# A hybrid decoder layer: head drawn into the ordered first stage, six merge products with gates ahead of the copies, other PSUM side for the FFN, last row tile in two column parts

## The chip, the cores and the metric

The program runs on one core of a Trainium2 chip. The metric is the device time of one execution in microseconds (us), lower is better. Beside times there is the trace of one profiled execution. Its engines are PE (TensorE, matmuls; PEld is its weight load), DVE (VectorE), ACT (ScalarE), POOL (GpSimd) and SP (SyncE, which here issues the transfers). Each engine takes its instructions in the order of its own queue, and waits at one whose inputs aren't ready.

## The reference, cut to what matters

One decoder layer on 512 tokens of width 1024: an input projection feeds two causal mixers, whose outputs are projected, gated by channel, merged, projected again, added to the input and normalized; then a gated FFN with a short convolution, and again a normalization.

```python
h = x @ w_in
y_a = nsa_attention(q, k.., v.., gates, ..) @ w_nsa_out        # 8 heads of 64, three branches
y_b = gated_deltanet(qkv, beta, decay, gate, ..) @ w_gdn_out   # 4 heads of 128, chunks of 64
gate_a, gate_b = split(merge_gate)                             # 2 x 1024 columns of h
mix = (sigmoid(gate_a) * y_a + sigmoid(gate_b) * y_b) @ w_o
x = layer_norm(ALPHA * x + mix, ln1_g, ln1_b)
gate, val = split(causal_dwconv(x @ w_up, conv_w))             # 2 x 2816 columns, width 3
x = layer_norm(ALPHA * x + (silu(gate) * val) @ w_down, ln2_g, ln2_b)
```

Everything is float32.

## The kernel before

**Products.** A float32 operand is split into a high part in the matmul type (float32r) and the rest (`xh`, `xl`; `wh`, `wl`). A product is three matmuls: high by high, high by low, low by high. Weights come by DMA into one of three `raw` buffers; `split_w` (L361) makes `wh` (mostly on ScalarE) and `wl` (VectorE or GpSimd), each with three buffers. `gemm_t(u)` (L396) is 24 matmuls of 512 columns into one of the two PSUM banks `pg`: unit u, 128 columns of the input projection, for all 512 tokens. Its weight is called `w<u>` in the order below (w20, w18, ...).

**The head.** After eight idle matmuls on zeros (`still`), `token_major` (L410) loads the eight x tiles (256 KB each) and four weight tiles `wB` (288 KB), splits them, and makes 96 matmuls of 288 columns into four banks `pb`, one for each tile of 128 tokens. They hold the columns that are wanted token by token (v, gates, decays); small copies take them out (`vcat`, `gsig`, `bd`). Then seven SyncE transfers bring constants: `cst` (722 KB), `ident` and small rows (L467 to L490). The Tile scheduler orders all this.

**The ordered stage.** From there to the end of both mixers, `draw(name, f)` runs a step only to record its instructions for each engine, and the loop at L1014 gives them out as the table `GIVEN` says: `w20S` is the next SyncE instruction of step w20, `q0P*12` twelve TensorE instructions of step q0, `n0V@2` the third VectorE instruction of n0. `PLACE` says which buffer each tile takes. Instructions of this stage have line L1023, of all others L252, since helpers make them. Merge products are steps of this stage too: `g0` to `g6` are seven of the 16 gate products; the gate itself (`gate`, a tanh on ScalarE that empties the pg bank into `mt`) belongs to the step for the first `BUFS["mg"]` = 5.

**The merge** (L1026 to L1075): eight outputs of the mixers (`oT`, `yT`) are copied to `yoh`, of which six on ScalarE, and the rests to `yol`. Behind these in the program stand the gates of products 5 and 6. Then, for each of m = 0..7: gate products, up to four ahead, two output products of 12 matmuls into the two banks `pm`, and their merging on VectorE and ScalarE into `mh`, `ml`; in between weights for `w_o` are split.

**Behind it**: `w_o` (tiles `pw`), transposes (`pt`), the first normalization; FFN-up with `pu`; FFN-down, where products of sums (`tdn` holds sums of weights, made through `traw` buffers and stored to DRAM) go into `pdna` and `pdnb`, four banks. `mul` (L1277) takes 11 blocks, loaded by twos; `early` puts the split weights of the first two into `wh`/`wl`, the others into `dh`/`dl`. At the end the last product is done for row tile 0 and then 1, six blocks each, followed by `add`, statistics and `norm`, which stores 512 columns twice.

PSUM has eight banks. Before: `pg` 0 and 1, `pb` 2 to 5, then `pd` 2 and 3, `pa` 4 to 6, `po` 7; `pm` 2 to 5; `pu` 0 to 3, `pw` 4 and 5, `pt` 6 and 7; `pdn` 4 to 7.

## Time and profile before

| | us |
|---|---|
| median of 3 runs (lowest, highest) | 832.1 (831.31, 832.76) |
| the profiled execution: whole time | 835.69 |
| its span | 833.9 |
| mean granted TensorE clock | 0.992 |

The span goes from the first to the last recorded instruction. The stages in the trace:

| stage | from, us | to, us |
|---|---|---|
| head | 0 | 20.9 |
| ordered stage | 20.9 | 328.4 |
| merge | 328.4 | 429.1 |
| w_o and first normalization | 429.1 | 484.0 |
| FFN-up | 484.0 | 718.5 |
| FFN-down | 718.5 | 825.8 |
| tail | 825.8 | 833.9 |

Rows of the profile name the line, the engine, the operation and the tiles, written left of `<-` and read right of it. "x48" is a count. In brackets stands the idle time ahead and what ended it.

### The profile page before, as it was taken

What the parts mean: (1) busy time and instruction counts of PE and PEld (TensorE: products, weight loads), DVE (VectorE), ACT (ScalarE), POOL (GpSimd) and SP (SyncE); (2) the same over time, 40 slices, a digit from 0 to 9 for tenths busy, and PEclk for the clock granted to TensorE, in tenths of its full rate; (3) what the DMA queues carried; (4) which work ended last, traced back from release to release, by engine and by line L of the source; (5) the groups of instructions that cost most, each with busy time, mean ns of one, the idle gap of its engine ahead of it and who ended that gap; (6) DMA issues with size and microseconds to landing.
All of it is one profiled execution on the core that took longest, in us unless ns stands there. A gap on an engine that the chain in (4) does not pass through costs nothing.

```text
span 833.9 us, 12016 instructions
## 1 busy us (share of the span) xinstructions
PE 813.7 (98%) x4226; PEld 685.5 (82%) x4226; DVE 636.8 (76%) x1373; ACT 403.8 (48%) x916; POOL 143.5 (17%) x127
## 2 busy tenths in 40 slices
...
GB/s 276 97 85 102 51 51 51 26 27 88 65 27 66 29 36 74 97 160 124 151 200 154 16 61 103 186 186 190 194 202 202 202 202 209 208 219 200 265 197 103
DMA packets 39820, 108.06 MB, mean 130 GB/s; under 512 B 4560, under 2 KB 4944, under 8 KB 39504
## 3 DMA queue, kind: packets, MB, share of 16 engines
...
q8 instruction: 33, 0.54, 0.3%
...
## 4 chain that ended last, share of the span: by engine, by line
PE 86%; DVE 6%; DMA 4%; ACT 2%; issue 2%; POOL 0%; SPq 0%; DVEq 0%; ACTq 0%; POOLq 0%
PE pu L252 27%; PE pg L1023 20%; PE pd L1023 7%; PE pg L252 6%; PE pa L1023 5%; PE pm L252 5%; PE pdna L252 5%; PE pdnb L252 4%; PE pw L252 3%; PE po L1023 3%; DMA raw<-in_down 2%; DVE x L252 1%; DVE wl L252 1%; DMA raw<-in_wT 1%; DMA big<-in_xT 1%
## 5 line engine op out<-in xcount | busy, mean ns | idle before, releaser
L252 PE MATMUL pu<-mh,wh 128*128 128x512 f32 (+1 forms) x384 | 142.7, 372 | 0.0
L252 PE MATMUL pu<-ml,wh 128*128 128x512 f32 (+1 forms) x384 | 142.6, 371 | 0.0
L252 PE MATMUL pu<-mh,wl 128*128 128x512 f32 (+1 forms) x384 | 142.6, 371 | 0.0
L252 ACT ACTIVATE wh<-raw 128x512 fp32r<-128x512 f32 (+2 forms) x120 | 75.5, 632 | 110.7 <-PE pu L252 70.0
L252 DVE TENSOR_TENSOR wl<-raw,wh 128x512 fp32r<-128x512 f32 (+2 forms) x116 | 93.7, 810 | 37.2 <-ACT wh L252 37.0
L1023 PE MATMUL pg<-xh,wh 128*128 128x512 f32 x248 | 100.2, 407 | 1.8 <-ACT wh L1023 1.8
L1023 PE MATMUL pg<-xl,wh 128*128 128x512 f32 x248 | 99.2, 401 | 0.0
L1023 PE MATMUL pg<-xh,wl 128*128 128x512 f32 x248 | 97.7, 399 | 0.0
L252 PEld LDWEIGHTS pu<-ml,wh 128*128 128x128 f32 x384 | 72.3, 188 | 12.6
L252 PEld LDWEIGHTS pu<-mh,wh 128*128 128x128 f32 x384 | 72.3, 188 | 12.6
L252 PEld LDWEIGHTS pu<-mh,wl 128*128 128x128 f32 x384 | 72.3, 188 | 12.3
L252 DVE SCALAR_TENSOR_TENSOR fa<-pu,fcw,fa 128x511 f32<-128x511 f32 x88 | 65.7, 746 | 9.3 <-ACT fa L252 7.9
L252 POOL TENSOR_TENSOR fth<-fth,fa 128x512 f32<-128x512 f32 x22 | 29.5, 1340 | 214.1 <-DVE fa L252 199.9
L252 DVE TENSOR_TENSOR dl<-raw,dh 128x512 fp32r<-128x512 f32 x69 | 46.6, 705 | 18.4 <-ACT dh L252 18.2
L252 ACT ACTIVATE dh<-raw 128x512 fp32r<-128x512 f32 x69 | 41.7, 627 | 35.4 <-DVE dl L252 10.4
L1023 PEld LDWEIGHTS pg<-xh,wh 128*128 128x128 f32 x248 | 47.1, 190 | 10.7 <-ACT wh L1023 2.0
L1023 ACT ACTIVATE big<-big,mn 128x384 f32<-128x384 f32 (+3 forms) x84 | 45.6, 554 | 21.1 <-DVE mn L1023 20.3
L1023 PEld LDWEIGHTS pg<-xh,wl 128*128 128x128 f32 x248 | 46.9, 190 | 8.9 <-DVE wl L1023 0.4
L1023 PEld LDWEIGHTS pg<-xl,wh 128*128 128x128 f32 x248 | 47.0, 189 | 8.3
L1023 POOL TENSOR_TENSOR wl<-raw,wh 128x512 fp32r<-128x512 f32 x28 | 36.3, 1306 | 80.6 <-ACT wh L1023 49.7
L252 POOL TENSOR_TENSOR rs<-rs,minus_half 128x1 f32<-128x1 f32 x8 | 7.5, 942 | 166.1 <-DVE rs L252 166.1
L252 PE MATMUL pg<-xh,wh 128*128 128x512 f32 x72 | 29.4, 408 | 5.3 <-ACT mt L252 5.3
...
## 6 DMA issues: line engine op xcount, KB each, us to landing
...
tdn<-traw SPq DMA_DIRECT2D x44, 256.0 KB, 3.1
...
```

Source lines behind the costliest of these rows:

```text
L252: return give(*a, **kw)
L1023: give(*a, **kw)
```

## The change

- The head is drawn too: `token_major(k0)` as steps t0, t2, t4, t6, the copies out of its banks as u, the constants as z; the table gives their places. The first x tile and the first wB tile come in halves, and for k0 = 0 VectorE makes the high part. The four accumulators are tiles of `pd` and `pa`.
- `GIVEN` and `PLACE` are new for the whole ordered stage; the steps in it are the same but for the head and the gate g5.
- `BUFS["mg"]` is 6: six gates belong to the ordered stage, and three gate products stand ahead of the first output product instead of two. The leftover gate (product 6) is written ahead of the yoh copies.
- `pu` lies on the right side of PSUM (banks 4 to 7), so `pw` takes the banks of `pg`, `pt` 2 and 3, `pdn` 0 to 3.
- FFN-down: blocks 2 and 3 of the first product go into tiles `eh`, `el` of a new pool `tl`, where the `traw` buffers were.
- The last row tile is multiplied in two halves of the last 512 columns, the second into a bank of its own; its statistics have three parts, its first normalizing pass is one operation of 1024 columns, the second three (512, 256, 256), each stored by itself.

Three places show the moved instructions. First SyncE, from the last x tile of the head on (`big` holds x tiles; the first `raw<-in_wT` is w20). Before:

```order
L252 DMA big7_94<-in_xT 128x512
L252 DMA cst_350<-in_consts 128x1444
L252 DMA ident_352<-in_consts 128x128
L252 DMA gcw_358<-in_gcw 128x48
L252 DMA fcw_360<-in_fcw 128x132
L252 DMA gnw_363<-in_gnw 128x1
L252 DMA alog_366<-in_glog 128x4
L252 DMA gdt_368<-in_gdt 128x4
L1023 DMA raw1_157<-in_wT 128x1024
```

The same place after the change:

```order
L1044 DMA big7_94<-in_xT 128x512
L1044 DMA raw1_157<-in_wT 128x1024
L1044 DMA gdt_208<-in_gdt 128x4
L1044 DMA raw2_158<-in_wT 128x1024
L1044 DMA gcw_204<-in_gcw 128x48
L1044 DMA raw0_156<-in_wT 128x1024
L1044 DMA raw1_157<-in_wT 128x1024
L1044 DMA raw2_158<-in_wT 128x1024
L1044 DMA pos_242<-in_pos 128x32
L1044 DMA alog_207<-in_glog 128x4
L1044 DMA raw1_157<-in_wT 128x1024
L1044 DMA cst_200<-in_consts 128x1444
```

w20 now follows x at once, and cst stands behind six weight loads. Second ScalarE, from the last copy of the ordered stage (`big<-po`) on; `mt` are gates. Before:

```order
L1023 ACTIVATE big22_109<-po0_398 64x512
L252 ACTIVATE yoh_3281<-oT_429 128x512
L252 ACTIVATE yoh_3281<-oT_432 128x512
L252 ACTIVATE yoh_3281<-yT_424 128x512
L252 ACTIVATE yoh_3281<-yT_426 128x512
L252 ACTIVATE yoh_3281<-yT_427 128x512
L252 ACTIVATE yoh_3281<-yT_435 128x512
L252 ACTIVATE mt_3311<-pg1_172 128x512
L252 ACTIVATE mt_3313<-pg0_171 128x512
```

And after the change:

```order
L1044 ACTIVATE big2_89<-po0_182 64x512
L1044 ACTIVATE mt_260<-pg0_183 128x512
L261 ACTIVATE mt_3285<-pg1_184 128x512
L261 ACTIVATE yoh_3279<-oT_253 128x512
L261 ACTIVATE yoh_3279<-oT_256 128x512
L261 ACTIVATE yoh_3279<-yT_248 128x512
L261 ACTIVATE yoh_3279<-yT_250 128x512
L261 ACTIVATE yoh_3279<-yT_251 128x512
L261 ACTIVATE yoh_3279<-yT_259 128x512
```

Both gates moved ahead of the six copies. Third ScalarE at the start of FFN-down (`dh`, `eh` are high parts of weights, `h` parts of the FFN's inner values, `fa` the last of FFN-up). Before:

```order
L252 ACTIVATE fa1_6232<-pu1_6207,fcw_360 128x512
L252 ACTIVATE dh_6281<-raw1_157 128x512
L252 ACTIVATE dh_6285<-raw1_157 128x512
L252 ACTIVATE dh_6302<-raw2_158 128x512
L252 ACTIVATE dh_6306<-raw2_158 128x512
L252 ACTIVATE h11_4488<-s3_4500 128x512
L252 ACTIVATE dh_6323<-raw0_156 128x512
L252 ACTIVATE h12_4490<-fth_6236 128x256
```

And after the change:

```order
L261 ACTIVATE fa1_6228<-pu1_6203,fcw_205 128x512
L261 ACTIVATE dh_6301<-raw2_158 128x512
L261 ACTIVATE eh2_6280<-raw1_157 128x512
L261 ACTIVATE eh3_6284<-raw1_157 128x512
L261 ACTIVATE dh_6305<-raw2_158 128x512
L261 ACTIVATE h11_4484<-s3_4496 128x512
L261 ACTIVATE dh_6322<-raw0_156 128x512
L261 ACTIVATE h12_4486<-fth_6232 128x256
```

Block 4's high part (first `dh<-raw2`) went ahead of those of blocks 2 and 3, which are `eh` now. The diff, with the two tables cut to a line or two and longer hunks to their core:

```diff
 GIVEN = """
-w20S w20A w20V w20A w20V n0V@2 q0P*12 w18S dV@2 dV@3 dA@1 w0S q0P*10 dV@4 dV@5 dV@6 w18A n2G@1 w18A w18V dV@7 w18V
...
+t0S@2 t0S@1 t0V@2 t0A@1 t0P@6 t0V@3 t0P@7 t0V@1 t0P@8 t0P@9 t0P@10 t0S t0A t0P@3 t0P@4 t0P@11 t0V t0P*3 t0S*2 t0V*2
+t0A t0V t0P t0P@15 t0P@16 t0P@21 t0P*4 t2S t2A t0P@22 t0P@23 t2S t2A t0P*3 t2P@6 t2V*2 t2S t2A@3 t2A t2V t2P@3 t2P@9
...
 """.split()
...
-BUFS = {...'mg': 5, 'mr': 4...}
+BUFS = {...'mg': 6, 'mr': 4...}
 PLACE = {
...
 }
...
     ps1 = ExitStack()
     psg = ExitStack()
     pg = psg.enter_context(tc.tile_pool(name="pg", bufs=BUFS["pg"], space=PSUM))
-    ps0 = ExitStack()
-    pb = ps0.enter_context(tc.tile_pool(name="pb", bufs=1, space=PSUM))
+    pd = ps1.enter_context(tc.tile_pool(name="pd", bufs=BUFS["pd"], space=PSUM))
+    pa = ps1.enter_context(tc.tile_pool(name="pa", bufs=BUFS["pa"], space=PSUM))
+    po = ps1.enter_context(tc.tile_pool(name="po", bufs=1, space=PSUM))
+    R.update({n: Places(p.tile, n, BUFS[n], S) for n, p in (("pd", pd), ("pa", pa), ("po", po))})
     R["pg"] = Places(pg.tile, "pg", BUFS["pg"], S)
...
-    def load_x(k):
+    def load_x(k, n=1, between=lambda: None):
         xr = R["big"].tile()
-        SP.dma_start(out=xr, in_=d["xT"][:, k, :])
-        A.activation(xh[:, k, :], xr, AF.Copy)
-        V.tensor_tensor(xl[:, k, :], xr, xh[:, k, :].bitcast(F32), op=OP.subtract)
-
-    def split_w(src, shape, eng, first=A):
-
-        raw = R["raw"].tile(shape)
-        SP.dma_start(out=raw, in_=src)
+        for i in range(n):
+            ts = slice(i * S // n, (i + 1) * S // n)
+            SP.dma_start(out=xr[:, ts], in_=d["xT"][:, k, ts])
+            if i == 0:
+                between()
+        for i in range(n):
+            ts = slice(i * S // n, (i + 1) * S // n)
+            A.activation(xh[:, k, ts], xr[:, ts], AF.Copy)
+            V.tensor_tensor(xl[:, k, ts], xr[:, ts], xh[:, k, ts].bitcast(F32), op=OP.subtract)
+
+    def split_w(src, shape, eng, first=A, raw=None):
+
+        if raw is None:
+            raw = R["raw"].tile(shape)
+            SP.dma_start(out=raw, in_=src)
...
-    def token_major():
-        pss = [pb.tile([128, 288], F32, name=f"pb{t}") for t in range(TT)]
-        for k0 in range(0, KD, 2):
+    def token_major(k0, pss):
+        if k0:
             load_x(k0)
             hi, lo = split_w(d["wB"][:, k0:k0 + 2, :], [128, 2, 288], V)
             load_x(k0 + 1)
-            for i in range(2):
-                k = k0 + i
-                wh, wl = hi[i], lo[i]
-                for t in range(TT):
-                    ts = slice(t * 128, (t + 1) * 128)
-                    PE.matmul(pss[t], xh[:, k, ts], wh, start=(k == 0), stop=False)
-                    PE.matmul(pss[t], xh[:, k, ts], wl, start=False, stop=False)
-                    PE.matmul(pss[t], xl[:, k, ts], wh, start=False, stop=(k == KD - 1))
+        else:
+            raw = R["raw"].tile([128, 2, 288])
+            load_x(0, 2, lambda: SP.dma_start(out=raw[:, 0], in_=d["wB"][:, 0]))
+            SP.dma_start(out=raw[:, 1], in_=d["wB"][:, 1])
+            hi, lo = split_w(None, [128, 2, 288], V, first=V, raw=raw)
+            load_x(1)
+        for i in range(2):
+            k = k0 + i
+            wh, wl = hi[i], lo[i]
+            for t in range(TT):
+                ts = slice(t * 128, (t + 1) * 128)
+                PE.matmul(pss[t], xh[:, k, ts], wh, start=(k == 0), stop=False)
+                PE.matmul(pss[t], xh[:, k, ts], wl, start=False, stop=False)
+                PE.matmul(pss[t], xl[:, k, ts], wh, start=False, stop=(k == KD - 1))
+
+    def token_parts(pss):
...
-    token_major()
-    ps0.close()
+    pss = [R[n].tile((128, 288)) for n in ("pd", "pd", "pa", "pa")]
+    for k0 in range(0, KD, 2):
+        draw(f"t{k0}", token_major, k0, pss)
+    draw("u", token_parts, pss)
...
+    def small_inputs():
+        SP.dma_start(out=cst, in_=d["consts"][:, 128:])
...
+    draw("z", small_inputs)
...
+    done = BUFS["mg"]
+    while done in MG:
+        gate(done, mg2)
+        done += 1
     yol = []
     for i in range(8):
         src = (oT + yT)[i]
         copy(E("yoh", i, "A"), yoh[:, i, :], src)
         yol.append(yo_tile("yol", F32R))
         E("yol", i).tensor_tensor(yol[i], src, yoh[:, i, :].bitcast(F32), op=OP.subtract)
-    done = BUFS["mg"]
-    while done in MG:
-        gate(done, mg2)
-        done += 1
...
-    def layer_norm(r, gb, st, after=lambda i: None):
+    def layer_norm(r, gb, st, after=lambda cs: None, first=(0, 512, 1024), second=(0, 512, 1024)):
         mv = ln.tile([128, 2], F32, name="mv", bufs=2)
         V.bn_aggr(out=mv, in_=st)
         rs = ln.tile([128, 1], F32, name="rs", bufs=2)
         V.tensor_scalar(rs, mv[:, 1:2], LN_EPS, None, op0=OP.add)
         rsqrt(rs, rs, 1)
-        for i in range(2):
-            cs = slice(i * 512, (i + 1) * 512)
+        for a, b in zip(first, first[1:]):
+            cs = slice(a, b)
             V.scalar_tensor_tensor(r[:, cs], r[:, cs], mv[:, 0:1], gb[:, 0, cs], op0=OP.subtract, op1=OP.mult)
+        for a, b in zip(second, second[1:]):
+            cs = slice(a, b)
             V.scalar_tensor_tensor(r[:, cs], r[:, cs], rs, gb[:, 1, cs], op0=OP.mult, op1=OP.add)
-            after(i)
+            after(cs)
     ps3 = ExitStack()
-    pu = psum("pu", 2)
+    pu = ctx.enter_context(tc.tile_pool(name="pu", bufs=2, space=PSUM, side="right"))
     pw = ps3.enter_context(tc.tile_pool(name="pw", bufs=1, space=PSUM))
     pt3 = ps3.enter_context(tc.tile_pool(name="pt3", bufs=2, space=PSUM))
...
         if p in WS:
             weight_sums(WS.index(p), done)
     tq.close()
+    tq = ExitStack()
+    tl = pool(tq, name="tl", bufs=1, side="left")
     mix.close()
     tw = ctx.enter_context(tc.tile_pool(name="tw", bufs=1, side="right"))
...
-    def mul(n, src, pss, more=False, to=NB, early=0):
+    def mul(n, src, pss, more=False, to=NB, early={}):
         for b0 in range(0, to, 2):
             k = min(2, to - b0)
-            hi, lo = weights(src, b0, k, wp if b0 < early else None)
+            hi, lo = weights(src, b0, k, early.get(b0))
             for j in range(k):
                 for i in range(2):
                     block(pss[i], n, b0 + j, i, (hi[j], lo[j]), b0 + j == 0 and not more, b0 + j == NB - 1)
             if work:
                 next(work[0], None)
-    stats = [ln.tile([128, 2, 6], F32, name=f"st{t}") for t in range(TT)]
+    stats = [ln.tile([128, 2 + (t == 1), 6], F32, name=f"st{t}") for t in range(TT)]
...
-    def norm(t):
+    def norm(t, **parts):
         ts = slice(t * 128, (t + 1) * 128)
         r = x1[:, t, :]
-        layer_norm(r, ln2, stats[t], lambda j: SP.dma_start(
-            out=out[ts, j * 512:(j + 1) * 512], in_=r[:, j * 512:(j + 1) * 512]))
+        layer_norm(r, ln2, stats[t], lambda cs: SP.dma_start(out=out[ts, cs], in_=r[:, cs]), **parts)
     pair = lambda n: [pdn.tile([128, S], F32, name=f"pdn{n}{i}") for i in range(2)]
     dn = d["down"]
     pa_, pb_ = pair("a"), pair("b")
-    mul("11", dn[:, 0, :, 0, :], pa_, early=2)
+    mul("11", dn[:, 0, :, 0, :], pa_, early={0: wp, 2: tl})
     for i in range(2):
         add(i, n2, pa_[i], True)
         add(2 + i, n1, pa_[i], True)
...
     pa_ = pair("a")
     mul("s1", tdn[0], pa_)
     work.clear()
+    tq.close()
     sums.close()
     lg = ctx.enter_context(tc.tile_pool(name="lg", bufs=1, side="left"))
     ln2 = lg.tile([128, 2, D], F32, name="ln2")
...
     for i in range(2):
         norm(2 + i)
     for i in range(2):
+        cut = 256 if i else 512
         for b, w in last:
-            block(pa_[i], "s4", b, i, w, False, b == NB - 1)
+            block(pa_[i][:, :cut], "s4", b, i, [x[:, :cut] for x in w], False, b == NB - 1)
         add(i, n2, pa_[i])
-        V.bn_stats(out=stats[i][:, 1, :], in_=x1[:, i, n2])
-        norm(i)
+        if i == 0:
+            V.bn_stats(out=stats[i][:, 1, :], in_=x1[:, i, n2])
+            norm(i)
+    rest = pdn.tile([128, S], F32, name="pdnb0")[:, 256:]
+    V.bn_stats(out=stats[1][:, 1, :], in_=x1[:, 1, 512:768])
+    for b, w in last:
+        block(rest, "s4", b, 1, [x[:, 256:] for x in w], b == last[0][0], b == NB - 1)
+    add(1, slice(768, 1024), rest)
+    V.bn_stats(out=stats[1][:, 2, :], in_=x1[:, 1, 768:])
+    norm(1, first=(0, 1024), second=(0, 512, 768, 1024))
```

227 lines of the change are left out of this document (114 added, 113 removed).

## The prediction

> **What bounds the kernel now.** I read the page first: the engines' busy times and the chain that ended last.
>
> ```profile
> span 833.9 us, 12016 instructions
> PE 813.7 (98%) x4226; PEld 685.5 (82%) x4226; DVE 636.8 (76%) x1373; ACT 403.8 (48%) x916; POOL 143.5 (17%) x127
> PE 86%; DVE 6%; DMA 4%; ACT 2%; issue 2%; POOL 0%; SPq 0%; DVEq 0%; ACTq 0%; POOLq 0%
> ```
>
> TensorE is busy for 98% of the span and carries 86% of the chain. The change removes no matmul (18 of 512 columns become 36 of 256). So the time can fall only where TensorE stands still or runs slowly. The view of TensorE's waits lists the first kind:
>
> ```profile
> PE pg L252 <- ACT mt L252: 5.3, 1, 5.3
> PE pg L1023 <- ACT wh L1023: 1.8, 1, 1.8
> PE pdna L252 <- DVE dl L252: 1.5, 1, 1.5
> PE pw L252 <- DVE mt L252: 0.8, 1, 0.8
> PE pt L252 <- DVE x L252: 0.4, 1, 0.4
> ```
>
> The columns are total, times and longest, in us. Each is one event. Windows laid around four of them, each pair being the wait and the stretch behind it, show the second kind (TensorE is the first busy time, its matmul count in brackets, and PEclk the granted clock):
>
> ```profile
> 18.95:20.89 1.94, 0.16 (x2) 0.00 (x0) 1.08 (x4) 1.61 (x12) 0.00 (x0) 1.00 0.65 244
> 20.89:25.50 4.61, 4.61 (x12) 3.38 (x13) 3.05 (x11) 1.36 (x5) 0.00 (x0) 0.63 0.42 121
> 327.90:333.76 5.86, 0.56 (x5) 0.26 (x3) 4.78 (x8) 4.10 (x9) 0.33 (x1) 0.91 0.07 27
> 333.76:339.60 5.84, 5.84 (x14) 4.58 (x15) 2.60 (x4) 2.01 (x3) 4.09 (x3) 0.51 0.01 3
> 428.80:430.10 1.30, 0.52 (x3) 0.10 (x2) 0.77 (x2) 0.00 (x0) 0.00 (x0) 1.00 0.31 50
> 430.10:434.00 3.90, 3.90 (x17) 3.23 (x18) 2.02 (x3) 2.46 (x3) 0.00 (x0) 1.00 0.92 352
> 725.50:727.45 1.95, 0.44 (x2) 0.01 (x1) 1.75 (x5) 1.95 (x6) 0.00 (x0) 1.00 0.45 137
> 727.45:731.00 3.55, 3.55 (x15) 2.93 (x16) 3.55 (x8) 1.95 (x4) 0.00 (x0) 1.00 0.27 12
> ...
> 374.85 10.88 PE pg L252 x48
> 477.17 5.75 PE pu L252 x48
> ```
>
> The last two rows, from the chain in order of time, give the price of a matmul without a wait: 10.88/48 = 0.227 us with 512 columns, 5.75/48 = 0.120 with 256. Behind the wait at 327.99, 14 matmuls took 5.84 us instead of 14 x 0.227 = 3.17: **2.7 us lost to a granted clock of 0.51**. Behind that at 18.95, 12 took 4.61 instead of 2.72: **1.9 us lost at 0.63**. Behind the two shorter waits the clock is 1.00 and nothing is lost (17 x 0.227 = 3.86 of 3.90). So idle time of 0.8 to 1.5 us costs itself, and of 1.8 us or more nearly the double.
>
> [...]
>
> **The head.** Rows of the timeline, TensorE, then ScalarE, then the chain:
>
> ```profile
> 10.35 0.35 PE L252 MATMUL pb<-wh,xh 128*128 128x288 f32 x1
> 11.07 0.40 PE L252 MATMUL pb<-wl,xh 128*128 128x288 f32 x1 [0.37 <-DVE wl L252]
> 18.82 0.29 PE L252 MATMUL pb<-wh,xl 128*128 128x288 f32 x1
> ...
> 9.29 0.63 ACT L252 ACTIVATE xh<-big 128x512 fp32r<-128x512 f32 x1 [1.26 <-DMA big<-in_xT]
> ...
> 13.39 6.74 DMA raw<-in_wT
> ...
> 0.00:20.90 20.90, 17.37 (x113) 16.32 (x113) 11.73 (x27) 11.93 (x31) 1.06 (x7) 1.00 0.83 275
> ```
>
> The 288-column matmuls take 0.132 us each (58 steps from 11.07 to 18.82 are 7.75 us). The last ends near 18.95. Then TensorE waits for the first weight of the ordered stage, w20, issued at 13.39 and landed at 20.13. Ahead of it on SyncE's queue stood cst (722 KB) and six small inputs. In the new order they stand behind it. At the 275 GB/s of the last row 722 KB are 2.6 us, so w20 lands by 17.5 even when issued as late as now; its hi part (ACT, 0.63) is there by 18.2.
>
> How much earlier does the head end? The halves let it begin a little earlier, but k=3 stands on the landing of its x tile (row at 9.29), whose bytes are no fewer, and so again begins at about 10.3. The new order puts three hi products ahead of the first that needs wl, which hides some 0.4 of the 0.7 us between 10.35 and 11.07. So the head ends at 18.5 (18.0 to 19.0), and w20's product follows at once, against 20.89: **-2.4 us** (-1.9 to -2.9). Without the idle time the slow stretch goes: **-1.9**. The copies out of the head's accumulators, 4 x 4 small ones, now lie among the first products; ScalarE and VectorE are busy 48% and 76% of the span, so they fit. cst, now issued behind five more weight loads, is first read for a score whose matmuls stand some 68 matmuls, 15.4 us, behind the head's end; I take no wait for it, and up to 2 us against.
>
> **The merge.** ScalarE around the long wait:
>
> ```profile
> 327.53 0.59 ACT L1023 ACTIVATE big<-po 64x512 f32<-64x512 f32 x1 [0.54 <-PE po L1023]
> 329.86 1.15 ACT L252 ACTIVATE yoh<-oT 128x512 fp32r<-128x512 f32 x2 [1.73 <-DVE oT L1023]
> 330.91 2.17 ACT L252 ACTIVATE yoh<-yT 128x512 fp32r<-128x512 f32 x4
> 333.11 1.09 ACT L252 ACTIVATE mt<-pg 128x512 f32<-128x512 f32 x2
> ...
> L252 PE MATMUL pg<-xh,wh 128*128 128x512 f32 x72 | 29.4, 408 | 5.3 <-ACT mt L252 5.3
> ```
>
> Both banks of pg hold finished products (5 and 6) whose gates stand behind six yoh copies, and these behind the last oT. Each bank's next user is a product of TensorE. In the new order the gate of product 5 comes right behind the copy big<-po, and the gate of product 6 ahead of the copies. TensorE's next product then waits only for the gate of the product it has just ended: a matmul's 0.4 to its end, 1.09/2 = 0.55 for the gate, 0.1 to the start (first gate ends near 333.66, TensorE starts 333.76), less the 0.23 of the normal step: 0.85, say 0.9 us. That is in the range that kept the clock (0.8 to 1.5). Three products (72 matmuls, 16.3 us) now stand ahead of the first pm, where there were two; they cover the six copies (3.3 us). The sum here is -5.3 - 2.7 + 0.9 = **-7.1** (-7.6 to -3.2). The upper end is that ScalarE's two copies ahead of the gate (a weight copy of 0.63 and big<-po of 0.59) are both late: 2.1 us of wait, and the 2.7 remain.
>
> **The first output product.** pw waited 0.8 us for VectorE to empty a pm bank. It now takes pg's banks, long free; what it needs beside weights is mh and ml of the last m, first read behind the products with the seven before. **-0.8**, and perhaps half of the 0.4 of pt, since VectorE's read of x is no longer behind: -0.2. Together -1.0 (-1.4 to -0.3).
>
> **FFN-down.**
>
> ```profile
> 719.76 2.18 ACT L252 ACTIVATE dh<-raw 128x512 fp32r<-128x512 f32 x4
> 724.73 0.63 ACT L252 ACTIVATE dh<-raw 128x512 fp32r<-128x512 f32 x1 [2.27 <-DMA raw<-in_down]
> 725.70 0.76 DVE L252 TENSOR_TENSOR l<-fth,h 128x256 fp32r<-128x256 f32 x2 [1.14 <-ACT h L252]
> 726.71 0.68 DVE L252 TENSOR_TENSOR dl<-raw,dh 128x512 fp32r<-128x512 f32 x1
> tdn<-traw SPq DMA_DIRECT2D x44, 256.0 KB, 3.1
> ```
>
> The wait of 1.5 is for block 5's dl at 726.71, which VectorE does behind l, which waits for h, which ScalarE does behind a dh that waits for a load. That chain stands in the new order as before. What is new is that blocks 2 and 3 lie where traw lay, so ScalarE's eh2 waits for the last tdn store. Behind it on ScalarE stand eh3, block 5's dh and the next weights; TensorE needs block 2 at 718.53 + 12 x 0.227 = 721.25. A store lands some 2 to 3 us after the subtraction that ends at 717.9, thus 719.9 to 721.0, and el2 comes 1.3 us later: up to 1 us of new wait, taken out of the 1.5 that follows. I take **0** (-1.2 to +0.8).
>
> **The tail.**
>
> ```profile
> 826.35 0.68 DVE L252 TENSOR_TENSOR x<-x,pdna 128x512 f32<-128x512 f32 x1
> 827.07 0.69 DVE L252 BATCH_NORM_STATS2 st<-x 128x6 f32<-128x512 f32 x1
> 828.11 1.40 DVE L252 SCALAR_TENSOR_TENSOR x<-x,mv,ln 128x512 f32<-128x512 f32 x2
> 829.43 1.41 DVE L252 SCALAR_TENSOR_TENSOR x<-x,rs,ln 128x512 f32<-128x512 f32 x2
> L252 DVE TENSOR_TENSOR s<-fth x22: 411/419/429, 499.1 to 724.2; 128x256 f32<-128x256 f32 x22
> ```
>
> VectorE goes without a gap from the last tile but one, so it, not TensorE, sets the end. A 512-column operation takes 0.69, a 256-column one 0.42. The last tile's add and statistics become 0.69 + 3 x 0.42 (was 2 x 0.69): +0.57; one first pass of 1024 columns instead of two saves some 0.15; two halves for the last 512 columns cost 0.15. VectorE ends 0.5 later, the last store carries half the bytes: **+0.1** (-0.3 to +0.6). TensorE's 18 x 0.227 become 36 x 0.120, +0.24, hidden behind VectorE.
>
> **The rest of the ordered stage** is planned anew. The trace shows only the old order:
>
> ```profile
> by line: PE pg L1023 54.1%; PE pd L1023 19.3%; PE pa L1023 15.1%; PE po L1023 7.7%; DVE row L1023 1.0%; DVE ptl L1023 0.7%; issue 0.5%; DVE big L1023 0.5%; POOL row L1023 0.3%; ACT big L1023 0.2%; ACT pth L1023 0.2%; DVE wl L1023 0.2%; DVE
> ```
>
> That is the chain from 25.5 to 327.9: 96.2% on TensorE, so 3.8% of 302.4, 11.5 us, in short waits. The work is the same but for one gate and the head's copies. Nothing says which way it goes: **0**, within a third of 11.5, +-4.
>
> **Sum.** -2.4 - 1.9 - 7.1 - 1.0 + 0 + 0.1 + 0 = **-12.3 us** on the profiled run's 835.69, thus 823.4. That run lies 3.6 above the median of the three times; taken from the median, 832.1 - 12.3 = **819.8**.
>
> **The rivals.**
> 1. *The merge's wait stays over 1.8 us* and the clock falls again, by the upper end above: 819.8 + 3.9 = 823.7. For it: ScalarE has two foreign copies ahead of the gate. Against: their inputs are ready eleven matmuls earlier. 0.12.
> 2. *The change doesn't do what it says at the head*: the transfers, at 0.83 of the engines until 20.9, not the order, set when w20 is there, so the product starts at 20.9 and the slow stretch stays: 819.8 + 4.3 = 824.1. 0.08.
> 3. *Slower*: the new order of the ordered stage makes TensorE wait behind copies on the in-order queues of ScalarE and VectorE. Each wait of the head's kind costs 1.8 + 1.9 = 3.7 us, so from four of them on (14.8 against 12.3) the kernel is slower, 834 or more; against it, the old order has none such between 25.5 and 327.9 in the list of waits. 0.05. With two or three it loses part: 827 to 831, 0.04.
> 4. *The head's slow stretch isn't the wait's* and stays, the 12 matmuls behind w20's landing being slow in any order: 821.7. 0.05. [...]
> 5. *The new order also waits less* in the ordered stage, by 4 to 8 of its 11.5: 812 to 816. 0.10.
>
> **Chances.** The forecast, 817 to 823, holds 0.53; with rivals 1, 2, 4 and 5 and the partial loss it makes faster by over 0.2% 0.92; slower by over 0.2% 0.05; between 0.03 (0.2%, 1.7 us, is about what a measurement of this kernel can tell from no change). The range 813.5 to 826.5 takes in rivals 1, 2 and 4, most of 5 and the unknown +-4 of the ordered stage.
>
> **What would show it.** In the changed profile: w20's product starts at about 18.5 with PEclk 1.00 from 18 to 25; TensorE's largest wait at the merge is near 0.9 and the window behind it has PEclk 1.00; no wait of pw for mt; the dl wait of FFN-down is about as long as now, split in two; VectorE's last operation ends 5.2 us after its add of the last tile. The prediction is wrong if the waits between 25 and 316 us leave 11.5 by more than 4, or a half-clock stretch stands anywhere.

## The result, and the profile after

| | before, us | after, us |
|---|---|---|
| median (lowest, highest), same chip | 831.7 (830.93, 832.76), 4 runs | 824.26 (823.9, 824.68), 4 runs |
| the profiled execution: whole time | 835.69 | 824.18 |
| its span | 833.9 | 822.4 |

The kernel became faster, by 7.4 us: the ratio is 0.991 (95% interval 0.9893 to 0.9927). The forecast was 819.8, which is 12.3 us below the 832.1 that it was taken from. The measured 824.26 lies outside the forecast's 817 to 823 and inside the wide range of 813.5 to 826.5. From one profiled execution to the other the difference is 11.5.

The page of the kernel after (engines' busy times, the chain that ended last), to be held against that of before:

```profile
span 822.4 us, 12070 instructions
PE 808.9 (98%) x4244; PEld 685.3 (83%) x4244; DVE 642.0 (78%) x1378; ACT 404.6 (49%) x915; POOL 144.8 (18%) x127
PE 91%; DVE 5%; ACT 1%; DMA 1%; issue 1%; SPq 0%; POOL 0%; POOLq 0%; DVEq 0%; ACTq 0%
```

TensorE now carries 91% of the chain, and DMA has gone from 4% to 1%. Its list of waits in the kernel after (total, times, longest, in us):

```profile
PE pg L261 <- DVE still L261: 1.0, 1, 1.0
PE pdna L261 <- DVE el L261: 0.9, 2, 0.7
PE pg L261 <- ACT mt L1044: 0.7, 1, 0.7
PE pd L1044 <- ACT big L1044: 0.7, 1, 0.7
```

The waits of 5.3, 1.8, 1.5 and 0.8 are no longer there; the merge's is 0.7. The windows of the kernel after, at the head's end and at the merge (columns: window, length, then busy time and count of PE, PEld, DVE, ACT and POOL, the granted clock, DMA share and GB/s):

```profile
18.91:21.00 2.09, 2.09 (x12) 1.69 (x11) 1.77 (x7) 1.13 (x7) 0.00 (x0) 1.00 0.05 20
21.00:25.50 4.50, 4.50 (x22) 3.72 (x21) 4.08 (x20) 2.89 (x9) 0.00 (x0) 1.00 0.47 133
324.30:325.60 1.30, 0.61 (x5) 0.30 (x3) 1.05 (x2) 0.65 (x2) 0.00 (x0) 1.00 0.00 0
325.60:331.40 5.80, 5.80 (x26) 4.79 (x27) 4.63 (x9) 4.51 (x9) 1.07 (x1) 1.00 0.01 3
```

The granted clock is 1.00 in all four: 26 matmuls take 5.80 us behind the merge's wait, where 14 took 5.84 before. Both slow stretches (granted clock 0.63 and 0.51 in the windows of before) have gone.

**Where the time went.** For this table I added up, in each trace, what every matmul took from its start to the next one's start beyond the step without a wait (0.227 us for 512 columns, 0.132 for 288, 0.120 for 256 and so on), counting only what is over 0.06 us. The third column is a second profiled execution of the unchanged kernel (the first experiment below). All in us:

| place in the trace | before, the profile shown | before, again | after |
|---|---|---|---|
| head, 0 to 25 | 5.7 | 3.5 | 2.0 |
| ordered stage, 25 to 300 | 15.0 | 15.0 | 15.0 |
| its end and the merge, 300 to 350 | 9.1 | 8.8 | 1.3 |
| first output product, 425 to 500 | 2.0 | 1.8 | 0.6 |
| FFN-down, 700 to 750 | 2.2 | 2.1 | 1.5 |
| sum of what TensorE lost | 33.9 | 31.1 | 20.4 |
| from the last matmul's start to the end | 8.6 | 8.6 | 9.8 |

The merge is the gain. The tail is a loss of 1.2. The head gave 3.7 against the first profile, but 1.5 against the second. Second profile against after, the table's sum is 31.1 - 20.4 - 1.2 = 9.5, the difference of the spans 831.0 - 822.4 = 8.6: 0.24 are the narrower matmuls of the tail, the rest is too small in each step for this count.

### The profile page after: what moved, and what is told of

Same layout as the page of the kernel before. It is cut to its first block, busy times and chain, and to the rows that moved or that the text cites. A ratio compares the mean times of both kernels' runs of the same rounds, so it can differ in the third digit from the quotient of the medians.

```text
span 822.4 us, 12070 instructions
## 1 busy us (share of the span) xinstructions
PE 808.9 (98%) x4244; PEld 685.3 (83%) x4244; DVE 642.0 (78%) x1378; ACT 404.6 (49%) x915; POOL 144.8 (18%) x127
## 4 chain that ended last, share of the span: by engine, by line
PE 91%; DVE 5%; ACT 1%; DMA 1%; issue 1%; SPq 0%; POOL 0%; POOLq 0%; DVEq 0%; ACTq 0%
PE pu L261 27%; PE pg L1044 20%; PE pd L1044 8%; PE pa L1044 6%; PE pg L261 6%; PE pw L261 5%; PE pm L261 5%; PE pdna L261 5%; PE pdnb L261 5%; PE po L1044 3%; DVE x L261 1%; DVE fa L261 1%; DVE el L261 1%; DVE big L1044 1%; DMA big<-in_xT 1%
## 5 line engine op out<-in xcount | busy, mean ns | idle before, releaser
L261 PE MATMUL pu<-mh,wh 128*128 128x512 f32 (+1 forms) x384 | 142.7, 372 | 0.0
L261 PE MATMUL pu<-ml,wh 128*128 128x512 f32 (+1 forms) x384 | 142.6, 371 | 0.0
L261 PE MATMUL pu<-mh,wl 128*128 128x512 f32 (+1 forms) x384 | 142.6, 371 | 0.0
L261 ACT ACTIVATE wh<-raw 128x512 fp32r<-128x512 f32 (+1 forms) x112 | 72.0, 646 | 96.2 <-PE pu L261 68.3
L261 DVE TENSOR_TENSOR wl<-raw,wh 128x512 fp32r<-128x512 f32 (+1 forms) x108 | 90.6, 841 | 32.1 <-ACT wh L261 32.0
L1044 PE MATMUL pg<-xh,wh 128*128 128x512 f32 x248 | 97.4, 398 | 0.0
L261 PEld LDWEIGHTS pu<-mh,wl 128*128 128x128 f32 x384 | 72.4, 188 | 12.6
L261 PEld LDWEIGHTS pu<-mh,wh 128*128 128x128 f32 x384 | 72.4, 188 | 12.5
L261 PEld LDWEIGHTS pu<-ml,wh 128*128 128x128 f32 x384 | 72.4, 188 | 12.4
L261 DVE SCALAR_TENSOR_TENSOR fa<-pu,fcw,fa 128x511 f32<-128x511 f32 x88 | 65.6, 746 | 9.3 <-ACT fa L261 7.9
L261 POOL TENSOR_TENSOR fth<-fth,fa 128x512 f32<-128x512 f32 x22 | 29.5, 1340 | 214.0 <-DVE fa L261 199.9
L261 DVE TENSOR_TENSOR dl<-raw,dh 128x512 fp32r<-128x512 f32 x67 | 44.0, 686 | 18.8 <-ACT dh L261 18.5
L261 ACT ACTIVATE dh<-raw 128x512 fp32r<-128x512 f32 x67 | 40.8, 627 | 34.7 <-DMA raw<-tdn 12.8
L1044 ACT ACTIVATE big<-big,mn 128x256 f32<-128x256 f32 (+3 forms) x84 | 46.1, 554 | 23.9 <-DVE mn L1044 22.1
L261 POOL TENSOR_TENSOR rs<-rs,minus_half 128x1 f32<-128x1 f32 x8 | 8.1, 1008 | 165.3 <-DVE rs L261 165.3
L1044 ACT ACTIVATE wh<-raw 128x512 fp32r<-128x512 f32 (+1 forms) x54 | 32.4, 607 | 9.1 <-PE pg L1044 5.0
```

Of the source, the lines that this page charges most:

```text
L261: return give(*a, **kw)
L1044: give(*a, **kw)
```

## The experiments

Times are medians with the lowest and the highest. Runs in one table ran on one chip beside the kernel before; the ratio is to that. The changed kernel wasn't timed again beside them. The kernel before has medians of 831.7 to 832.4 in these sets of runs, so a difference of less than 0.7 us from the changed kernel's 824.26 says little by itself.

| run | us | ratio (95% interval) |
|---|---|---|
| before_again | 832.36 (830.86, 833.69) | 1.0001 (0.9993 to 1.001) |
| gates_only | 827.82 (826.85, 829.78) | 0.9948 (0.9935 to 0.996) |
| tail_undone | 822.8 (822.64, 823.54) | 0.9885 (0.9872 to 0.9898) |
| cst_first | 825.69 (823.93, 826.36) | 0.9914 (0.9903 to 0.9926) |
| kernel before beside these four | 832.38 (830.38, 833.37) | |

| run | us | ratio (95% interval) |
|---|---|---|
| mg6_before | 824.52 (823.7, 825.17) | 0.9911 (0.9897 to 0.9925) |
| tl_undone | 823.54 (822.87, 823.97) | 0.9899 (0.9884 to 0.9914) |
| pu_left | 824.98 (823.95, 825.57) | 0.9918 (0.9903 to 0.9933) |
| tail_two | 823.48 (822.65, 824.32) | 0.9899 (0.9883 to 0.9915) |
| kernel before beside these four | 832.13 (829.63, 833.06) | |

| run | us | ratio (95% interval) |
|---|---|---|
| best1 | 823.24 (822.98, 823.66) | 0.9897 (0.9884 to 0.9911) |
| g6_inside | 824.78 (823.98, 824.99) | 0.9914 (0.99 to 0.9927) |
| x_whole | 824.82 (823.55, 826.29) | 0.9915 (0.9902 to 0.9929) |
| kernel before beside these three | 831.8 (831.37, 832.35) | |

The last, el_pool, ran alone: 822.78 (822.18, 822.85), ratio 0.9885 (0.9866 to 0.9905), beside a kernel before at 832.16 (830.4, 834.22).

### Was the profiled execution of before a typical one? before_again

No edit. Theory A: the forecast's terms came from an execution that was slower than the usual one, and some of them aren't there otherwise.

> The kernel before, unchanged, for its spans and clocks in several executions and for a second profile. What is to be explained: in the two profiles the span fell from 833.9 to 822.4 (11.5 us, 12.3 foretold), in the medians the time fell by only 7.4 (831.7 to 824.26); the profiled execution of before was 4.0 us above its own median, that of the changed kernel at its median. Theory A (the clock differs by execution): the waits of 5.3 and 1.8 us are in every execution, but the half-speed stretches behind them (4.6 us lost in the profile) are not, or are shorter; then most spans lie near 830 at a mean clock of 0.995 or more, and a profile at 830 shows the same waits and PEclk near 1.0 behind at least one of them. Theory B (transfers differ by execution): the clock is 0.992 in every execution and the 4 us are missing in some wait for a DMA, FFN-down's load of 5.5 us first.

The same windows, head and merge, in this second profile of the unchanged kernel (whole time 832.82, span 831.0):

```profile
18.70:20.30 1.60, 0.26 (x2) 0.14 (x2) 1.19 (x4) 1.60 (x12) 0.00 (x0) 1.00 0.75 292
20.20:25.00 4.80, 4.80 (x20) 3.66 (x21) 3.96 (x14) 2.05 (x6) 0.00 (x0) 1.00 0.31 116
331.35:337.20 5.85, 5.85 (x14) 4.61 (x15) 2.61 (x4) 2.01 (x3) 4.11 (x3) 0.53 0.01 3
```

The wait for w20 is 1.5 us here, not 1.94, and behind it the clock is 1.00: no slow stretch. The merge is as before, 14 matmuls in 5.85 us at 0.53. So theory A holds for the head and not for the merge: the 1.9 us of the head's slow stretch, and some 0.4 of its wait, belonged to that one execution. Two things on record bear this out: gates_only and mg6_before (below) have the unchanged head too, with a wait of 1.3 in their lists and no drop; and the first profile's 835.69 lies above every other time of the unchanged kernel here (829.63 to 834.22). Theory A's sign of a mean clock of 0.995 or more didn't come. The mean is 0.992 in both, but it also counts the idle end behind the last matmul, where a drop costs nothing: the clock is at half there for the last 6.0 us of before_again and for the last 2.9 of the first profile.

The wait itself isn't what the prediction took it for. ScalarE's row for the high part of w20 in the first profile, then in before_again with the row ahead of it:

```profile
20.21 0.63 ACT L1023 ACTIVATE wh<-raw 128x512 fp32r<-128x512 f32 x1 [0.33 <-DMA raw<-in_wT]
```

```profile
19.42 0.17 ACT L252 ACTIVATE bd<-pb 128x8 f32<-128x8 f32 x1
19.48 0.63 ACT L1023 ACTIVATE wh<-raw 128x512 fp32r<-128x512 f32 x1
```

In the first profile ScalarE is idle until the transfer has landed, at 20.13. In before_again w20 has landed at 18.91, but ScalarE is busy from 17.67 on with ten copies out of the head's accumulators, which stand ahead of the split in its queue. It is the same in gates_only and mg6_before: landed at 19.32 and 17.82, split at 19.89 and 19.85, without idle time ahead. So in three of the four profiles of this head the wait for w20 ends with ScalarE's copies, and not with the transfer.

### The merge: gates_only, mg6_before, g6_inside

In gates_only the kernel before gets one edit of the change, the leftover gates (here of products 5 and 6) ahead of the copies:

```diff
+    done = BUFS["mg"]
+    while done in MG:
+        gate(done, mg2)
+        done += 1
     yol = []
     for i in range(8):
...
-    done = BUFS["mg"]
-    while done in MG:
-        gate(done, mg2)
-        done += 1
```

> The kernel before with one edit: the loop that runs the leftover gates (products 5 and 6) is written ahead of the yoh copies. The order of the first stage, BUFS and all else are those of before. Theory A: the wait of 5.3 us shrinks to 0.5 to 1.0 us, no slow stretch behind it in any execution; the time falls by 4.5 to 5 in the median, where the slow stretch was mostly absent, and the profile's span by up to 7.5 against 833.9. If the replanning with a sixth gate inside the ordered stage was needed: less than 2 us.

It gains 4.6 us, which is about the size expected, but not by the expected way (a wait of 0.5 to 1.0 and no slow stretch). The gates as its timeline has them on ScalarE, with the idle time ahead in brackets:

```profile
327.88 1.08 ACT L252 ACTIVATE mt<-pg 128x512 f32<-128x512 f32 x2 [1.73 <-DVE oT L1023]
328.85 1.15 ACT L252 ACTIVATE yoh<-oT 128x512 fp32r<-128x512 f32 x2
```

TensorE's timeline and then the window behind its wait, in the same run:

```profile
328.53 0.50 PE L252 MATMUL pg<-xh,wh 128*128 128x512 f32 x1 [2.04 <-ACT mt L252]
```

```profile
328.50:335.00 6.50, 6.47 (x21) 5.19 (x22) 3.52 (x7) 5.16 (x9) 2.56 (x2) 0.74 0.01 3
```

The copies are no longer ahead, but the gate now waits 1.73 us for the last oT on VectorE. TensorE's wait falls from 5.3 to 2.0 and no further, and the clock still drops: 21 matmuls take 6.47 us instead of 21 x 0.227 = 4.77, so 1.7 are lost. Why a gate that reads only pg waits for oT isn't shown by a run; the likely reason is that its tile `mt` comes from a pool (`mg2`) laid where the ordered stage's memory is given back, which is at its end.

mg6_before adds to gates_only the other half, the gate of product 5 within the ordered stage:

```diff
-y3A*2 f71P g6P*2 f71P f73P*7 f75A f73P f75V g6P*11 w30V g6P*6 f74A f75P f74V f75P y3A y3V*4 g6P y3G g6P*3 y3V f75P*8
+y3A*2 f71P g6P*2 f71P f73P*7 f75A f73P f75V g6P*11 w30V g6P*6 g5A f74A f75P f74V f75P y3A y3V*4 g6P y3G g6P*3 y3V f75P*8
...
-BUFS = {...'mg': 5, 'mr': 4...}
+BUFS = {...'mg': 6, 'mr': 4...}
```

> The kernel before with three edits: the leftover gate ahead of the yoh copies (as in gates_only), BUFS mg 6, and the gate of product 5 put into the old order right behind its last matmul. All else, the head and the rest of the order too, is that of before. Theory: in gates_only the first gate still waited 1.73 us for VectorE's last oT, since a gate written behind the ordered stage gets memory that this stage gives back at its end; a gate inside the stage has its own. Then product 7 finds its bank free, TensorE waits at most 0.3 us at the merge, and no slow stretch follows: 5.5 + 2.7 us less than before, 823.5 to 825. Rival (replanning the whole order was needed): the wait stays near 2 us, about 828 as gates_only.

824.52, which is 7.6 below the kernel before: with these three small edits the kernel before is as fast as the changed one (824.26). Its window over the merge, and then its list of waits:

```profile
326.00:334.00 8.00, 8.00 (x38) 6.64 (x36) 5.93 (x9) 5.37 (x11) 2.50 (x2) 1.00 0.05 20
```

```profile
PE pg L1023 <- ACT wh L1023: 1.3, 1, 1.3
PE pg L252 <- DVE still L252: 1.0, 1, 1.0
PE pw L252 <- DVE mt L252: 0.8, 1, 0.8
```

TensorE is busy in all 8.00 us. The leftover gate still waits for oT (1.72 us), but no longer with TensorE behind it, since the other bank's gate is done and one more product can go there. What is left is the head's wait and that of pw, which the other parts of the change remove. By the table above they are worth 1.5 and 1.2, against 1.2 that the tail costs and a wait of 0.9 that the changed kernel keeps at the merge, so they nearly cancel.

Whether the leftover gate has to stand ahead of the copies at all, once product 5's gate is inside, wasn't run. An estimate from this run's ScalarE rows (leftover gate at 327.85, six copies until 331.57) says hardly: behind the copies the gate would end near 331.6, and TensorE begins the product that needs its bank at 331.77.

g6_inside makes the changed kernel do it the other way round, product 6's gate inside and product 5's behind:

```diff
-y3V f74A g5P*6 f74V f75A f75V f75P*6 g5P*2 f75P*2 y3G f75P*2 y3V*2 y3P y2P y3P*2 y2P*3 y2V y3P g5P f75A f75V g5A y3V
+y3V f74A g5P*6 f74V g6A f75A f75V f75P*6 g5P*2 f75P*2 y3G f75P*2 y3V*2 y3P y2P y3P*2 y2P*3 y2V y3P g5P f75A f75V y3V
...
-    done = BUFS["mg"]
-    while done in MG:
-        gate(done, mg2)
-        done += 1
+    gate(5, mg2)
+    done = 7
```

> The changed kernel with the gate of merge product 6 inside the ordered stage and that of product 5, which ends last, behind it. TensorE's next product then finds the bank of product 6 free and needn't wait for the gate of the product that it has just ended. If that wait (0.94 us in the profile) is what the merge still costs: 0.7 to 1.0 us faster than the changed kernel, the wait for mt gone, and the clock unchanged. Rival (product 7's weights or the copies aren't ready earlier): within 0.3.

824.78: no gain. The wait for `mt` (0.7) is gone from the list, and this line has come in its place:

```profile
PE pg L261 <- DVE wl L261: 1.1, 1, 1.1
```

TensorE now comes earlier to product 8, the second behind the ordered stage, and waits at 334.21 for the low part of its weight. The 0.9 us at the merge can't be taken by the gate's order alone.

### The head: cst_first, x_whole

cst_first puts the constants' transfers ahead of w20 again, as before the change, and leaves the head drawn:

```diff
-t6P@7 t6V t6A t6P@4 t6P t6P@11 t6V t6P@8 t6P@18 t6P@5 t6P@19 t6P@20 t6P*5 t6P@21 t6P*4 w20S uA@8 w20A w20V w20A uA@2
+t6P@7 t6V t6A t6P@4 t6P t6P@11 t6V t6P@8 t6P@18 t6P@5 t6P@19 t6P@20 t6P*5 t6P@21 t6P*4 zS zS zS zS zS zS zS w20S uA@8 w20A w20V w20A uA@2
```

> The changed kernel with its seven transfers of constants (cst of 722 KB first) issued ahead of w20, as before; the rest of the order is untouched. If these transfers set when w20 lands, w20's product starts at 20 to 21 as before, and TensorE waits 1.5 to 2 us: 1.5 to 2.0 us slower than the changed kernel without a slow stretch, 3.3 to 3.8 with one. Theory A expects the two amounts in different executions. Rival (the head's gain came from elsewhere, the split of the first tiles or the drawn order): within 0.3 us of the changed kernel.

825.69, 1.4 more than the changed kernel, though the runs overlap. The expectation (w20's product at 20 to 21, 1.5 to 2.0 us slower) was missed by a little. The last product of the head and w20's first, in cst_first:

```profile
18.36 0.29 PE L1044 MATMUL pa<-wh,xl 128*128 128x288 f32 x1
19.50 0.49 PE L1044 MATMUL pg<-xh,wh 128*128 128x512 f32 x1 [0.84 <-ACT wh L1044]
```

And in the changed kernel:

```profile
18.91 0.29 PE L1044 MATMUL pa<-wh,xl 128*128 128x288 f32 x1
19.04 0.39 PE L1044 MATMUL pg<-xh,wh 128*128 128x512 f32 x1
```

With the constants ahead a wait for w20 comes back; without them the product follows at its normal step of 0.13 us. The order of the transfers causes this wait: w20 lands at 18.80 here and at 16.82 in the changed kernel. But at 19.50 against 19.04 the profile shows 0.5 of the 1.4; another 0.6 was lost in FFN-down in this execution (2.1 where the table has 1.5), which the edit doesn't touch. So the median's 1.4 is not all the edit's.

Nor is the order of the transfers the whole of the head's gain. In before_again w20 landed about as in cst_first (18.91), and its product began at 20.16 instead of 19.50. The difference is in ScalarE's queue, where the new order puts only one small copy ahead of the split. Its row in the changed kernel:

```profile
18.00 1.14 ACT L1044 ACTIVATE wh<-raw 128x512 fp32r<-128x512 f32 x2
```

No run leaves the copies ahead and moves the transfers alone. Over all profiles w20's product starts at 20.16 to 20.89 in the four with the unchanged head and at 18.46 to 19.50 in the eight with the changed one.

x_whole loads the first x tile and the first wB tile whole again, with the table's step t0 fitted to it:

```diff
-            load_x(0, 2, lambda: SP.dma_start(out=raw[:, 0], in_=d["wB"][:, 0]))
-            SP.dma_start(out=raw[:, 1], in_=d["wB"][:, 1])
+            load_x(0, 1, lambda: SP.dma_start(out=raw, in_=d["wB"][:, 0:2, :]))
```

> The changed kernel with the first x tile and the first wB tile loaded whole. My step on the head said that starting earlier brings little, since the fourth x tile's landing sets the further pace: within 0.4 us of the changed kernel, TensorE's first matmul of the head at 4.9 to 5.2 instead of 4.47. Rival (the earlier start is worth its 0.5 us): 0.4 to 0.7 slower. [...]

824.82, within the spread of 824.26. The first matmuls of the head, one row of each kernel, x_whole first:

```profile
5.04 0.37 PE L960 MATMUL pa<-wh,xh 128*128 128x288 f32 x1 [0.42 <-DVE wh L960]
...
6.28 0.30 PE L960 MATMUL pa<-wh,xh 128*128 128x288 f32 x1
6.41 0.29 PE L960 MATMUL pa<-wl,xh 128*128 128x288 f32 x1
```

```profile
4.47 0.59 PE L1044 MATMUL pa<-wh,xh 128*128 128x288 f32 x1
...
6.06 0.44 PE L1044 MATMUL pd<-wl,xh 128*128 128x288 f32 x1
6.30 0.44 PE L1044 MATMUL pa<-wh,xl 128*128 128x288 f32 x1
6.54 0.43 PE L1044 MATMUL pd<-wh,xh 128*128 128x288 f32 x1
```

With the halves the head begins 0.57 us earlier, but in this profile its first ten matmuls step by 0.24 us, until about 6.8, where x_whole steps by 0.13 from 6.28 on. The halves aren't the reason: tail_undone has the same head with halves, steps by 0.13 from 4.63 on, and then stands still for 1.4 us until a later x tile has been split. w20's product starts at 19.04 in the changed kernel, at 18.84 in tail_undone and at 18.95 in x_whole. So the profiles show no gain from the halves; the medians leave a few tenths open.

### PSUM sides and the FFN's extra pool: pu_left, tl_undone

```diff
-    pu = ctx.enter_context(tc.tile_pool(name="pu", bufs=2, space=PSUM, side="right"))
+    pu = psum("pu", 2)
```

> The changed kernel with pu on the left side of PSUM as before, so that pw again takes banks which pm had. If the other side is what removed the wait of pw: a wait of 0.8 us for mt at the first pw matmul is back, 0.8 to 1.2 us slower than the changed kernel. Rival (the later merge products left VectorE earlier): within 0.3 us.

824.98, 0.7 more than the changed kernel, with ranges that overlap; the wait itself is back in the list, as before the change:

```profile
PE pw L261 <- DVE mt L261: 0.8, 1, 0.8
```

tl_undone takes the pool `tl` away from blocks 2 and 3 of FFN-down:

```diff
-    mul("11", dn[:, 0, :, 0, :], pa_, early={0: wp, 2: tl})
+    mul("11", dn[:, 0, :, 0, :], pa_, early={0: wp})
```

> The changed kernel with blocks 2 and 3 of FFN-down back in the buffers of before (no tiles where traw was). In the profile of the changed kernel TensorE waits 0.9 us for el there, and the 1.1 to 1.5 us for block 5's dl is gone. If the one is the price of the other: 0.3 us slower (0 to 0.8), the el wait gone and the dl wait back. Rival (the dl wait went because a transfer landed earlier, by chance): 0.5 to 0.9 faster.

The one long wait of before returns, `PE pdna L261 <- DVE dl L261` with 1.2 us, and TensorE's last matmul starts 0.62 us later than in the changed kernel (813.21 against 812.59). Yet the median is 823.54, 0.7 below it, where 0.3 above was expected. The reason for the sign is in VectorE's rows. First the changed kernel, then tl_undone, at the last weights of FFN-down (blocks 5 and 6, `el`):

```profile
797.87 1.29 DVE L261 TENSOR_TENSOR el<-raw,eh 128x512 fp32r<-128x512 f32 x2 [1.52 <-ACT eh L261]
```

```profile
797.27 1.29 DVE L261 TENSOR_TENSOR el<-raw,eh 128x512 fp32r<-128x512 f32 x2 [0.29 <-ACT eh L261]
```

From this operation on VectorE works almost without a gap to the end in both (a wait of 0.4 for `rs` near the end, and in tl_undone one of 0.2 for TensorE), so the end is set by when the load of these two blocks has landed. It landed at 797.19 in the one and 796.58 in the other (issued at 792.30 and 792.92, so it took 4.9 and 3.7 us). The issue is 0.62 later in tl_undone, as much as TensorE is late: what TensorE saves does reach VectorE's run, through this issue, but here a load that took 1.2 us longer used it up. That is hardly chance: the same load took 4.4 to 5.1 us in seven of the eight profiles with the pool (3.6 in pu_left) and 3.5 to 4.1 in all six without it. How the pool does it isn't shown, and what it costs in all isn't settled: the two ratios, 0.9899 and 0.991, have overlapping intervals.

### The tail: tail_undone, tail_two, el_pool

tail_undone is the changed kernel with the tail of before (last row tile whole, 512 columns at a time):

```diff
     for i in range(2):
-        cut = 256 if i else 512
         for b, w in last:
-            block(pa_[i][:, :cut], "s4", b, i, [x[:, :cut] for x in w], False, b == NB - 1)
+            block(pa_[i], "s4", b, i, w, False, b == NB - 1)
         add(i, n2, pa_[i])
-        if i == 0:
...
-    norm(1, first=(0, 1024), second=(0, 512, 768, 1024))
+        V.bn_stats(out=stats[i][:, 1, :], in_=x1[:, i, n2])
+        norm(i)
```

> The changed kernel with the end of the kernel before: the last row tile in one piece of 512 columns, two statistics, two passes of 512 each. The profiles show 8.5 us from the last matmul's start to the end before and 9.8 after, of which VectorE's chain from the last add is 4.5 and 5.5. If that is the price of the two column parts: 1.0 to 1.3 us faster than the changed kernel, about 823.1, and the chain from the last add back at 4.5. Rival (the halves hide work behind TensorE, and the longer end is the order of transfers): 0.3 slower.

822.8, which is 1.5 less, with no run in common with the changed kernel's range. The traces give the column parts 1.06 of it, as follows; the first add shown below also came 0.50 earlier, which isn't the tail's doing. VectorE's end of the changed kernel, from the last row tile's first add:

```profile
813.95 0.68 DVE L261 TENSOR_TENSOR x<-x,pdna 128x512 f32<-128x512 f32 x1
814.66 0.43 DVE L261 BATCH_NORM_STATS2 st<-x 128x6 f32<-128x256 f32 x1
815.01 0.40 DVE L261 TENSOR_TENSOR x<-x,pdnb 128x256 f32<-128x256 f32 x1
815.45 0.43 DVE L261 BATCH_NORM_STATS2 st<-x 128x6 f32<-128x256 f32 x1
...
816.25 1.28 DVE L261 SCALAR_TENSOR_TENSOR x<-x,mv,ln 128x1024 f32<-128x1024 f32 x1
817.96 1.54 DVE L261 SCALAR_TENSOR_TENSOR x<-x,rs,ln 128x512 f32<-128x512 f32 x3 [0.43 <-POOL rs L261]
```

And of tail_undone:

```profile
813.45 0.68 DVE L261 TENSOR_TENSOR x<-x,pdna 128x512 f32<-128x512 f32 x1
814.16 0.69 DVE L261 BATCH_NORM_STATS2 st<-x 128x6 f32<-128x512 f32 x1
...
815.21 1.40 DVE L261 SCALAR_TENSOR_TENSOR x<-x,mv,ln 128x512 f32<-128x512 f32 x2
816.53 1.41 DVE L261 SCALAR_TENSOR_TENSOR x<-x,rs,ln 128x512 f32<-128x512 f32 x2
```

From that add to the last operation's end it is 819.50 - 813.95 = 5.55 us with the parts and 817.94 - 813.45 = 4.49 without. Of the 1.06, 0.43 is a wait that wasn't there: GpSimd makes the one column `rs` (a power of 128x1) while VectorE is in its one operation of 1024 columns. GpSimd's row in the changed kernel, then in tail_two, where the first pass is again two operations of 512:

```profile
816.48 1.45 POOL L261 TENSOR_TENSOR rs<-rs,minus_half 128x1 f32<-128x1 f32 x1 [4.04 <-DVE rs L261]
```

```profile
817.13 0.92 POOL L261 TENSOR_TENSOR rs<-rs,minus_half 128x1 f32<-128x1 f32 x1 [4.04 <-DVE rs L261]
```

The edit of tail_two:

```diff
-    norm(1, first=(0, 1024), second=(0, 512, 768, 1024))
+    norm(1, first=(0, 512, 1024), second=(0, 512, 1024))
```

> The changed kernel with the last row tile still multiplied and added in two column parts, but both normalizing passes in two operations of 512 columns, as before. In the changed kernel's profile VectorE waits 0.43 us for GpSimd's rs between the one pass of 1024 columns (1.28 us) and the second pass; two operations (1.40) would cover more of that. If so: 0.2 to 0.4 us faster than the changed kernel. With the tail of before wholly back it was 1.5 faster (822.8 against 824.26), so the greater part stays with the parts of the add and the statistics. Rival (most of the 1.5 us is the third store and the wait): 1.0 or more faster.

823.48, 0.8 below the changed kernel (0.2 to 0.4 was expected), with ranges that overlap. The wait for `rs` is gone and the chain from the add is 5.04 us, so about half of the 1.06 was the long operation and the third store's piece; the other half is the add and the statistics in pieces.

el_pool asks whether VectorE's unbroken run can be shortened: tail_undone, with the low parts of the last four blocks made by GpSimd.

```diff
-            V.tensor_tensor(wl, raw[:, i], wh.bitcast(F32), op=OP.subtract)
+            (G if pl is not None and b0 >= 7 else V).tensor_tensor(wl, raw[:, i], wh.bitcast(F32), op=OP.subtract)
```

> tail_undone (the fastest so far, 822.8) with one edit: the low parts of the last four weight blocks (7 to 10, in el) are made by GpSimd instead of VectorE. Theory: in every profile VectorE works without a gap from the low parts of blocks 5 and 6 on to its last operation, some 21 to 24 us, so VectorE and not TensorE sets the end, and what is added to it there (the changed kernel's column parts) counts in full. Taking 2.5 us off it then moves the end until TensorE's last matmul sets it: VectorE waits for TensorE at both last adds, and the kernel is 0.5 to 1.0 us faster than tail_undone, about 822.0. Rival (TensorE sets the end already, or GpSimd slows VectorE as much as it takes off): within 0.3.

822.78 against 822.8: no gain. VectorE has lost its operation `el x4` of 2.48 us, and its next pass has grown. Its row, in el_pool, and GpSimd's beside it:

```profile
803.14 3.47 DVE L261 SCALAR_TENSOR_TENSOR x<-x,rs,ln 128x512 f32<-128x512 f32 x2
...
802.92 3.14 POOL L261 TENSOR_TENSOR el<-raw,eh 128x512 fp32r<-128x512 f32 x2
```

The same two operations of VectorE take 1.41 elsewhere in the tail, so 2.06 us of the 2.48 are given back while GpSimd works. VectorE's run from `el` to the last add is 813.65 - 797.92 = 15.73 us instead of 813.45 - 797.37 = 16.08, and it began 0.55 later.

### A version from the parts: best1

tail_undone, tl_undone and g6_inside in one kernel (the three diffs above).

> The changed kernel with three of its parts undone or mended: the tail of before, FFN-down's blocks 2 and 3 in the buffers of before, and the gate of product 6 (instead of 5) inside the ordered stage, as in g6_inside. If the three are separate: 1.46 (tail) + 0.72 (FFN-down) + 0.9 (wait for the gate) less than the changed kernel's 824.26, thus 821.2 (820.8 to 821.8), with no wait for mt at the merge. If the waits only move to the next one: 822 or more.

823.24 instead of the 821.2 expected: the sum of the parts didn't come. The gate's order brought the wait for `wl` (1.1), as in g6_inside, and the dl wait is back with 1.4. The best two kernels stay tail_undone and el_pool with 822.8, which is 9.4 to 9.6 below the kernel before on their chips and 1.5 below the changed one.

## Why the prediction was right and wrong

The sign was right, the time was 4.5 us off, next to the times of rivals 1 (823.7) and 2 (824.1), neither of which happened; only the traces tell them apart. The steps in turn; "measured" is the second profile of before against after, by the table above, unless a run is named.

| step | forecast | measured |
|---|---|---|
| head: wait, and slow stretch | -2.4, -1.9 | -1.5 |
| merge | -7.1 | -7.5; mg6_before -7.6 in the medians |
| first output product | -1.0 | -1.2; pu_left, its part undone, +0.7 |
| FFN-down | 0 | TensorE -0.6, used up by a slower load |
| tail | +0.1 | +1.2; tail_undone, the old tail, -1.06 in the trace |
| ordered stage | 0 | 0 |

**The step that failed** is in the sum: "That run lies 3.6 above the median of the three times; taken from the median, 832.1 - 12.3". A part of what made that execution long was among the terms. Its head had a wait of 1.94 with a slow stretch behind; before_again has 1.5 and none. The same gain was taken off a median in which it was not contained. That is 4.3 - 1.5 = 2.8 of the 4.5. The prediction noted the 3.6, but didn't ask which of its terms were a part of them.

The tail, below, is another 1.1. The rest isn't accounted for step by step: the table's steps add up to 9.5, the spans differ by 8.6, and the medians by 7.4 to 8.1, depending on which median of the kernel before is taken.

Held against its own execution the sum looks nearly right, -12.3 forecast and -11.5 found. That is in part luck, since errors cancel: by the table the head gave 3.7 for 4.3, the merge 7.8 for 7.1, the output product 1.4 for 1.0, FFN-down 0.7 for nothing, and the tail took 1.2 for 0.1. Two slips in the working are too small to matter: 7.75/58 is 0.134 and not 0.132, and the merge's wait adds up to 0.82 and not 0.85.

**The tail was mis-sized**, by 1.1. The 256-column pieces were right (0.43 and 0.40 against 0.42). Two terms failed. "One first pass of 1024 columns instead of two saves some 0.15": the pass is 1.40 - 1.28 = 0.12 shorter, and costs 0.43 of wait for `rs`, which the old profile couldn't show. And "the last store carries half the bytes" was to give back most of the 0.5 that VectorE ends later; from VectorE's end to the span's it is 822.4 - 819.50 = 2.9 us with 128 KB and 820.9 - 817.94 = 3.0 with 256 KB. So 0.1 came back.

**The merge was right in mechanism and size.** Forecast was a wait of 0.9 with no clock drop; TensorE's step into the first leftover product is 0.93 us longer than normal, and the list calls it 0.7. Moving the leftover gates alone isn't enough: gates_only gets 4.6 of 7.6. The gate inside the ordered stage alone wasn't run. ScalarE's rows in the changed kernel show why the forecast's upper end didn't come:

```profile
323.06 0.63 ACT L261 ACTIVATE wh<-raw 128x512 fp32r<-128x512 f32 x1 [2.27 <-PE pg L1044]
323.76 0.59 ACT L1044 ACTIVATE big<-po 64x512 f32<-64x512 f32 x1
324.86 0.60 ACT L1044 ACTIVATE mt<-pg 128x512 f32<-128x512 f32 x1 [0.51 <-PE pg L1044]
```

Both foreign copies are done 0.5 us before product 5 ends. Rival 1 falls.

**The head's mechanism was half right.** The transfers did what was foretold: w20 landed at 16.82 (forecast: by 17.5) and its product follows the head at once, so rival 2 falls, and cst_first shows that w20's place among the transfers counts. But "Then TensorE waits for the first weight of the ordered stage", landed at 20.13, describes the first profile only. In the other three profiles of the unchanged head w20 has landed earlier, and ScalarE's copies set the wait. The prediction saw these copies move and asked only whether they fit behind the head. The new order moves both; what each is worth alone wasn't run. The head's end was foretold at 18.5 (18.0 to 19.0); the product starts at 19.04 here, and at 18.46 to 19.50 in the eight profiles of this head.

**Rival 4**, that the head's slow stretch isn't the wait's and comes in any order, falls by before_again, gates_only and mg6_before: with a shorter wait at the same place (1.3 us in the list of each, against 1.8 in the profile of before) the granted clock behind it is 1.00 and the stretch is gone, though the order is the same. gates_only has a slow stretch elsewhere, at the merge, and there too it stands behind a wait, of 2.04 us.

**FFN-down** was costed as TensorE's waits. It got 0.6 less of them, and tl_undone shows that this wasn't worth anything here: VectorE's run to the end starts with a load, and with the new pool that load took longer. The prediction knew that "it, not TensorE, sets the end", but used it for the tail alone. **The ordered stage** came out as taken: 15.0 before and after, so rivals 3 and 5 fall. That its new order would change nothing was a guess (the prediction: "Nothing says which way it goes").
